# A hybrid transformer step on one Trainium2 core: one modulation vector's sums move from TensorE to VectorE, and the adaLN norms go over to whole tiles

## The chip, the cores and the metric

The kernel runs as one program on one core of a Trainium2 chip. A core has TensorE (matmuls into PSUM), VectorE, ScalarE, GpSimd and SyncE; each works through its own queue in order, and they wait for one another by semaphores. The metric is the device time of one execution in microseconds (us); lower is better. All data is fp32. A matmul of full precision is made of three passes over operands that are split into a high and a low part.

## The reference, cut to what matters

```python
for d in range(DEPTH):                                   # 2 layers, D_MODEL 1024
    mod = silu(c) @ w_mod[d] + b_mod[d]                  # 6 vectors of 1024, for each token group
    sa, ca, ga, sm, cm, gm = split(mod, 6)               # shift, scale, gate: mixer, then MLP
    h = rmsnorm(x, norm_mix[d]) * (1 + ca) + sa
    q, k, v, gb, gc, xin, u, vs = split(h @ w_in[d])
    x = x + ga * (concat(attention, conv, chunk_mlp) @ w_out[d])
    h = rmsnorm(x, norm_mlp[d]) * (1 + cm) + sm
    x = x + gm * (square(relu(h @ w_up[d])) @ w_down[d]) # hidden 4096
y = rmsnorm(x, norm_final)
```

There are two token groups, 128 context tokens modulated by `c_ctx` and 256 latent tokens modulated by `c`: 384 columns in all. A modulation vector is named here by layer and place in the split: (0, 3) is layer 0's MLP shift `sm`, (0, 5) its MLP gate `gm`.

## The kernel before, in words

Activations lie transposed: 1024 features are KT = 8 tiles `dt` of 128 partitions, by T = 384 tokens. `GROUPS` are the two token groups, columns 0 to 127 and 128 to 383.

**Weights.** `refill` loads a chunk of 128x1024 weights into `raw` (a ring of six buffers, which all streamed data shares), ScalarE rounds it to `whi`, VectorE subtracts to get `wlo` (four buffers each). `mm3` is one tile product in three matmuls: high by high, high by low, low by high. A chunk gives 24 matmuls of 384 columns.

**Order.** The four compute engines run in the order of the code. `tick()` is called after each `mm3`; side work is written as generators that yield a number of ticks (`WAIT`, one number for each layer) and are resumed when so many ticks have gone by. The order is thus fixed when the program is built, and an instruction whose data is late stops its engine.

**Modulation vectors.** Those in `MOD_PE` are made on TensorE by `mod_products`: 32 small matmuls `pm` of 256 columns for a vector, 8 of them in a step, then a transpose and `mod_done` on VectorE. Those in `MOD_DVE` are made on VectorE by `mod_sums`: `steps(sums, n, every)` issues n sums of 128x1024 (`junk`, with an accumulated result `mr`), one in `every` ticks, 16 for a vector; after the 16th comes `mod_done`.

**A layer.** Mixer: norm, input projections (`pkq`, then the 512 columns of `nat`, then `pgc`, `pxi`, `pgb`, `pk`, `pq`, `pu`), attention in twelve units (`sc` scores, `e` softmax, `pt` transposes, `po` values), output projection (`po2`). Then the MLP in two halves f = 0, 1: sixteen hidden tiles up (`pup`), eight output tiles down (`pdn`).

**Norms.** The first products of a norm run on x times scale, unnormed (`raw_x`, with two more columns that hold the shift: `shift_columns`), and `hidden` or `evict` multiplies by `rstd` afterwards. Meanwhile the true normed input (`normed_x`, tiles `nh`, `nl`, shown as `hh`, `hl`) is made tile by tile: in layer 1's mixer by `norm_part`, which calls `normed`, and during the down products of f = 0 by `normed_again`. For each tile VectorE makes `t` = x * scale * rstd in two instructions (one for each token group), ScalarE adds the shift and rounds into `hh` in two, VectorE makes the low part `hl` in two.

Of the kernel before, what the change touches and what calls it, by code (L numbers as in the profile page):

```python
# [21 lines left out]
T = TP + TS  # L22
# [13 lines left out]
    "sums_down": (6, 2),  # L36
    "hid0": (1, 3),
    "hid1": (3, 4),
    "later": (2, 3),
    "later2": (6, 6),  # L40
    "spread": (1, 1),
    "final": (4, 3, 3, 3),
# [9 lines left out]
    "at8": (1, 3),  # L52
    "at9": (2, 3),
    "at10": (3, 4),
    "at11": (3, 1),
    "at12": (1, 3),
    "k0": (1, 5),
    "k1": (8, 6),
# [9 lines left out]
    "cv1": (1, 2),  # L68
    "cv2": (2, 3),
    "cm0": (1, 1),  # L70
    "sy": (2, 1),
    "normed": (3, 3),
    "wait_normed": (13, 13),
    "mix": (6, 4),
# [1 line left out]
    "mods": (7, 0),  # L76
    "mods0": (5, 3),
    "sums": (7, 0),
    "sums0": (58, 1),
    "unit0": (24, 24),  # L80
    "head": (24, 24),
    "late": (0, 5),
# [2 lines left out]
GROUPS = ((0, 0, TP), (1, TP, T))  # L85
# [11 lines left out]
TE = T + 2  # L97
# [3 lines left out]
def dit_kernel(ctx, tc, xT, cT, wmod, wmodT, wall, wfirst, ck, cv, ws, lam, bs_in, small, rope, ident_in, yT, kT_out, v_out):  # L101
    nc = tc.nc
    const = ctx.enter_context(tc.tile_pool(name="const", bufs=1))
    wpool = ctx.enter_context(tc.tile_pool(name="wpool", bufs=1))
    work = ctx.enter_context(tc.tile_pool(name="work", bufs=2))
# [105 lines left out]
    def misc_tile(name="misc"):  # L211
        return ps.tile([P, 512], F32, tag="misc", name=name, bufs=3)

    def temp(name):
        return work.tile([P, T], F32, name=name, tag="tA", bufs=4)

    def mm3(out, w, a, wsl, asl, first, last):

# [110 lines left out]
    products = mod_products()  # L329
# [16 lines left out]
    def rsqrt_refined(y, a, ms):  # L346

        nc.vector.tensor_mul(a, y, y)
        nc.vector.scalar_tensor_tensor(a, a, -0.5, ms, ALU.mult, ALU.mult)
        nc.vector.scalar_tensor_tensor(y, a, 1.5, y, ALU.add, ALU.mult)  # L350

    def rstd_of_x():
        pm = misc_tile("pstat")
        mm(pm[:, 0:T], ones_d, stat["acc"], start=True, stop=True)
        y = stat["rstd"] = work.tile([P, T], F32, name="rstd", bufs=1)
        yield 2
        nc.scalar.activation(y, pm[:, 0:T], AF.Ln)
        nc.scalar.activation(y, y, AF.Exp, scale=-0.5)
        yield 2
        a = work.tile([P, T], F32, name="rtmp", tag="rtmp", bufs=1)  # L360
        rsqrt_refined(y, a, pm[:, 0:T])

    def normed(scale, shift, every):


        def times(dt):
            t = temp("t")
            for g, a, b in GROUPS:
                nc.vector.scalar_tensor_tensor(
                    t[:, a:b], x[:, dt, a:b], scale[:, dt, g : g + 1], stat["rstd"][:, a:b], ALU.mult, ALU.mult  # L370
                )
            return t

        t = times(0)
        for dt in range(KT):
            for g, a, b in GROUPS:
                nc.scalar.activation(nh[:, dt, a:b], t[:, a:b], AF.Identity, bias=shift[:, dt, g : g + 1])  # L377
            ahead = times(dt + 1) if dt + 1 < KT else None
            for g, a, b in GROUPS:
                nc.vector.scalar_tensor_tensor(  # L380
                    nl[:, dt, a:b], t[:, a:b], shift[:, dt, g : g + 1], nh[:, dt, a:b].bitcast(F32),
                    ALU.add, ALU.subtract,
                )
            t = ahead
            if dt + 1 < KT:
                yield every

    def normed_again(scale, shift, every):

        for dt in range(KT):  # L390
            t = temp("t")
            for g, a, b in GROUPS:
                nc.vector.scalar_tensor_tensor(
                    t[:, a:b], x[:, dt, a:b], scale[:, dt, g : g + 1], stat["rstd"][:, a:b], ALU.mult, ALU.mult
                )
            yield every[0]
            for g, a, b in GROUPS:
                nc.scalar.activation(nh[:, dt, a:b], t[:, a:b], AF.Identity, bias=shift[:, dt, g : g + 1])
            yield every[1]
            for g, a, b in GROUPS:  # L400
                nc.vector.scalar_tensor_tensor(
                    nl[:, dt, a:b], t[:, a:b], shift[:, dt, g : g + 1], nh[:, dt, a:b].bitcast(F32),
                    ALU.add, ALU.subtract,
                )
            yield every[2]

    def scaled_high(dt, scale, to=raw_x):
# [127 lines left out]
    for d in range(DEPTH):  # L535
# [125 lines left out]
        else:  # L661
# [10 lines left out]

            def norm_part():
                yield wt["wait_normed"]
                yield from normed(amix[d], modv[d][:, 0], wt["normed"])

            start(norm_part())
            for i in (2, 3):
# [229 lines left out]
        if d == 0:  # L908
            nc.sync.dma_start(bs, bs_in)
            for i in range(DEPTH):  # L910
                start(lambdas(i), 4 + 4 * i)
            start(steps(products, 3 * (KT // 2 + 1), wt["mods"]), wt["mods0"])
            start(steps(sums, 2 * KT, wt["sums"]), wt["sums0"])

        def units(h):
# [20 lines left out]
            chunk_mlp(ct)  # L936


        shift_columns(modv[d][:, 3])
        ya = (y[:, 0], y[:, 1])  # L940
        for i0 in range(0, KT, 2):
            outs = proj_tiles(ya, 2, T, "po2", (4, 5, 6, 0, 1, 2, 7, 3))
            for i in range(2):
                go(finish_x(i0 + i, outs[i], modv[d][:, 2], amlp[d]))

# [3 lines left out]
        for f in range(2):  # L949
            if d == 0:  # L950
                start(steps(sums, (16, 28)[f], (8, 4)[f]), 2)
            ah = wpool.tile([P, HALF, T], F32R, tag="hidH", name="ah")
            al = wpool.tile([P, HALF, T], F32R, tag="hidL", name="al")

            def hidden(i, pt, wait=0):
                if wait:
                    yield wait
                r = temp("relu")
                if f == 1:
                    nc.scalar.activation(r, pt[:, 0:T], AF.Relu)  # L960
                    nc.scalar.activation(r, r, AF.Square)
                    nc.scalar.copy(ah[:, i], r)
                    yield wt["hid1"]
                    nc.vector.tensor_sub(al[:, i], r, ah[:, i].bitcast(F32))
                    return
                ub = work.tile([P, 2], F32, name="ub")
                nc.vector.tensor_copy(ub, pt[:, T:TE])
                nc.vector.tensor_mul(r, pt[:, 0:T], stat["rstd"])
                yield wt["hid0"]
                for g, s0, s1 in GROUPS:  # L970
                    nc.scalar.activation(r[:, s0:s1], r[:, s0:s1], AF.Relu, bias=ub[:, g : g + 1])
                nc.scalar.activation(r, r, AF.Square)
# [12 lines left out]
            if f == 1 and not last:
                shift_columns(modv[d + 1][:, 0])
            if d == 0:
                start(steps(sums, (12, 24)[f], (9, 5)[f]), 2)
            if f == 0:
                start(normed_again(amlp[d], modv[d][:, 3], (2, 2, 12)), 3)  # L990

            def down(pt, w, c, cols):

                for k in range(8):
                    kt = c * 8 + k
                    mm3(pt[:, cols], w, (ah, al), (slice(None), slice(k * P, k * P + P)),
                        (slice(None), kt, cols), kt == 0, kt == HALF - 1)
                    tick()

            for dt in range(KT - 1 if last else KT):  # L1000
                pt = acc_tile("pdn")
                for c in range(2):
                    down(pt, chunk(), c, slice(0, T))
                    go(refill())
                go(finish_x(dt, pt, modv[d][:, 5], amix[d + 1] if f == 1 and not last else None, last))


    gate = modv[DEPTH - 1][:, 5]
    y = work.tile([P, T], F32, name="rstd", bufs=1)
    newton = work.tile([P, T], F32, name="rtmp", tag="rtmp", bufs=1)  # L1010

    def finish_part(dt, group, pt):
# [37 lines left out]

MOD_PE = ((0, 1), (0, 0), (0, 2), (0, 3), (0, 4))
MOD_DVE = ((0, 5), (1, 1), (1, 0), (1, 2), (1, 3), (1, 4), (1, 5))

_OUTS = [((KT, P, T), "float32"), ((DEPTH, NH, P, TP), "float32"), ((DEPTH, TP, 512), "float32")]

# [111 lines left out]
```

## Time and profile before

| | us |
|---|---|
| median of 3 runs (896.75 to 897.56) | 897.35 |
| the profiled execution | 896.73 |
| span of its records | 894.9 |
| TensorE busy in the span | 875.6 |
| VectorE busy | 657.3 |
| ScalarE busy | 485.7 |
| GpSimd busy | 82.8 |

An engine's busy time is the time in which at least one of its instructions runs. The profiled execution is 1.8 us longer than its span and 0.6 us shorter than the median. In the trace PE is TensorE, DVE VectorE, ACT ScalarE, POOL GpSimd.

### The profile page before, as it was taken

The page shows a single profiled execution, that of the slowest core. Times are in us where ns is not written, and L with a number is a line of the kernel's source. Part 1 is how long each engine was busy: PE and PEld are TensorE (multiplying, and loading weights), DVE is VectorE, ACT ScalarE, POOL GpSimd, SP SyncE. Part 2 cuts the span into 40 slices and gives each one's busy share as a digit, 9 for nine tenths or more (in the row PEclk, how much of TensorE's full clock was granted, in tenths as well). Part 3 has the DMA queues.
Part 4 walks back from the last instruction along what each step waited for, and adds up shares of the span by engine and source line. Part 5 has one row for each costly group of instructions (what it writes and reads, how often), then busy time and mean ns, then how long its engine had stood idle before and what let it go on. Part 6 is the DMA issues. An engine that isn't in the chain of part 4 may idle for free.

```text
span 894.9 us, 14560 instructions
## 1 busy us (share of the span) xinstructions
PE 875.6 (98%) x5502; PEld 840.4 (94%) x5502; DVE 657.3 (73%) x1218; ACT 485.7 (54%) x954; POOL 82.8 (9%) x85
## 2 busy tenths in 40 slices
PE   8999999999999999999999899999999999999996
PEld 6767889999999999999997799999999999999996
DVE  4699987889888779969979887568977554444332
ACT  4568775547654336554336786545765344565331
POOL 1015110020000000000112330002000000000022
PEclk9999999999999999999999999999999999999999
DMA  9976874455656558857663332233565343343302
GB/s 342 402 248 237 281 270 169 136 161 188 210 168 208 167 168 252 252 190 246 217 216 124 112 98 96 95 109 127 191 195 179 121 137 119 125 135 118 118 1 71
DMA packets 49046, 156.55 MB, mean 175 GB/s; under 512 B 5456, under 2 KB 11088, under 8 KB 48976
## 3 DMA queue, kind: packets, MB, share of 16 engines
q1 hardware_dynamic: 48432, 155.36, 52.5%
q8 instruction: 43, 0.70, 0.3%
q10 hardware_dynamic: 544, 0.26, 0.1%
q14 instruction: 27, 0.22, 0.1%
HBM read 152.98 MB, written 2.62 MB: 174 GB/s over the span
## 4 chain that ended last, share of the span: by engine, by line
PE 85%; DVE 6%; DMA 5%; issue 2%; ACT 1%; SPq 0%; POOL 0%; DVEq 0%; POOLq 0%; ACTq 0%
PE pdn L221 10%; PE pdn L220 10%; PE pdn L222 10%; PE pup L221 10%; PE pup L220 10%; PE pup L222 10%; PE po L221 2%; PE po L222 2%; PE po L220 2%; DMA raw<-in_wmod_dram 2%; PE po L823 1%; DVE wlo L203 1%; PE pm L264 1%; DVE hl L380 1%; DMA raw<-in_wall_dram 1%
## 5 line engine op out<-in xcount | busy, mean ns | idle before, releaser
L201 ACT CAST whi<-raw 128x1024 fp32r<-128x1024 f32 x182 | 190.0, 1050 | 276.0 <-PE pdn L221 114.0
L203 DVE TENSOR_TENSOR wlo<-raw,whi 128x1024 fp32r<-128x1024 f32 x182 | 222.8, 1230 | 80.2 <-ACT whi L201 80.0
L220 PE MATMUL pdn<-ah,whi 128*128 128x384 f32 (+2 forms) x528 | 174.9, 331 | 0.0
L221 PE MATMUL pdn<-al,whi 128*128 128x384 f32 (+2 forms) x528 | 174.8, 331 | 0.0
L222 PE MATMUL pdn<-ah,wlo 128*128 128x384 f32 (+2 forms) x528 | 174.8, 331 | 0.0
L220 PE MATMUL pup<-hh,whi 128*128 128x386 f32 (+1 forms) x512 | 173.7, 339 | 0.0
L221 PE MATMUL pup<-hl,whi 128*128 128x386 f32 (+1 forms) x512 | 172.8, 337 | 0.3
L222 PE MATMUL pup<-hh,wlo 128*128 128x386 f32 (+1 forms) x512 | 172.5, 337 | 0.0
L322 DVE SCALAR_TENSOR_TENSOR junk<-raw,cb 128x1024 bf16<-128x1024 f32 x112 | 136.5, 1219 | 0.7
L221 PEld LDWEIGHTS pdn<-al,whi 128*128 128x128 f32 x528 | 99.3, 188 | 0.0
L220 PEld LDWEIGHTS pdn<-ah,whi 128*128 128x128 f32 x528 | 99.2, 188 | 0.0
L222 PEld LDWEIGHTS pdn<-ah,wlo 128*128 128x128 f32 x528 | 99.3, 188 | 0.0
L221 PEld LDWEIGHTS pup<-hl,whi 128*128 128x128 f32 x512 | 96.5, 188 | 1.1 <-DVE hl L414 0.9
L220 PEld LDWEIGHTS pup<-hh,whi 128*128 128x128 f32 x512 | 96.2, 188 | 0.3
L222 PEld LDWEIGHTS pup<-hh,wlo 128*128 128x128 f32 x512 | 96.4, 188 | 0.0
L344 POOL TENSOR_TENSOR sacc<-sacc,sq 128x384 f32<-128x384 f32 x23 | 29.4, 1277 | 666.4 <-ACT sq L337 531.8
L425 DVE SCALAR_TENSOR_TENSOR x<-pdn,modv,x 128x128 f32<-128x128 f32 (+1 forms) x62 | 23.0, 413 | 46.8 <-PE pdn L222 46.6
L220 PE MATMUL po<-y,whi 128*128 128x384 f32 x128 | 43.1, 337 | 0.0
L222 PE MATMUL po<-y,wlo 128*128 128x384 f32 x128 | 42.8, 335 | 0.0
L221 PE MATMUL po<-y,whi 128*128 128x384 f32 x128 | 42.8, 334 | 0.0
L477 PE MATMUL nat<-whi,hl 128*128 128x512 f32 (+1 forms) x96 | 33.1, 345 | 2.4 <-DVE hl L380 2.3
L475 PE MATMUL nat<-whi,hh 128*128 128x512 f32 (+1 forms) x96 | 33.9, 354 | 0.5 <-ACT hh L377 0.5
(213 smaller groups left out, 1443.6 us busy)
## 6 DMA issues: line engine op xcount, KB each, us to landing
raw<-in_wall_dram SPq DMA_DIRECT2D x182, 512.0 KB, 3.6
raw<-in_wmodT_dram SPq DMA_DIRECT2D x56, 512.0 KB, 4.2
raw<-in_wmod_dram SPq DMA_DIRECT2D x40, 512.0 KB, 6.1
raws<-in_wfirst_dram SPq DMA_DIRECT2D x8, 256.0 KB, 7.4
x<-in_xT_dram SPq DMA_DIRECT2D x8, 192.0 KB, 6.5
raws<-in_wall_dram SPq DMA_DIRECT2D x2, 512.0 KB, 7.5
out_dram<-x SPq DMA_DIRECT2D x4, 256.0 KB, 2.3
mix<-in_cv_dram SPq DMA_DIRECT2D x2, 256.0 KB, 5.3
```

Of the source, the lines that this page charges most:

```text
L201: nc.scalar.copy(hi, r)
L203: nc.vector.tensor_sub(lo, r, hi.bitcast(F32))
L220: mm(out, wh[wsl], ah[asl], start=first, stop=False)
L221: mm(out, wh[wsl], al[asl], start=False, stop=False)
L222: mm(out, wl[wsl], ah[asl], start=False, stop=last)
L264: mm(pm[32 * j : 32 * j + 32, own], sct[:, kt, :], w[:, (4 * k + j) * width : (4 * k + j + 1) * width], start=(kt == 0), stop=(kt == KT - 1),)
L322: nc.vector.scalar_tensor_tensor(junk, w, 1.0, cb[:, g], ALU.mult, ALU.mult, accum_out=mr[:, dt, g : g + 1])
L344: eng.tensor_add(stat["acc"], stat["acc"], sq)
L380: nc.vector.scalar_tensor_tensor(nl[:, dt, a:b], t[:, a:b], shift[:, dt, g : g + 1], nh[:, dt, a:b].bitcast(F32), ALU.add, ALU.subtract,)
L425: nc.vector.scalar_tensor_tensor(x[:, dt, a:b], pacc[:, a:b], gate[:, dt, g : g + 1], x[:, dt, a:b], ALU.mult, ALU.add)
L475: mm(o, ah, wh[:, cols], start=(kt == 0 and tt % n == 0), stop=False)
L477: mm(o, al, wh[:, cols], start=False, stop=(kt == KT - 1 and (tt % n == n - 1 or tt == 2)))
```

## The change

(0, 3) goes from `MOD_PE` to the head of `MOD_DVE`. The sixteen sums that run during layer 0's mixer, (0, 5) before, are now (0, 3); (0, 5) moves to f = 0's up products, and layer 0's f = 0 down products carry 28 sums, one in 4 ticks, where they carried 12, one in 9. `shift_columns` for the MLP moves from before the output projection to after its third pair of tiles. `normed_again` and layer 1's mixer norm (`normed_whole`, new) multiply a whole tile by `rstd` on VectorE, apply scale and shift in place on ScalarE, round the whole tile there with one more instruction, and subtract the whole tile on VectorE. `hidden` takes the two shift columns through the same multiply as the tile (`rstd1`, with ones in its last two columns), without a copy of its own. Layer 0's mixer norm keeps `normed`.

```diff
-    "later": (2, 3),
+    "later": (2, 4),
-    "at11": (3, 1),
+    "at11": (4, 1),
-    "sy": (2, 1),
+    "sy": (4, 1),
...
-        y = stat["rstd"] = work.tile([P, T], F32, name="rstd", bufs=1)
+        stat["rstd1"] = work.tile([P, TE], F32, name="rstd", bufs=1)
+        nc.gpsimd.memset(stat["rstd1"][:, T:TE], 1.0)
+        y = stat["rstd"] = stat["rstd1"][:, 0:T]
...
+    def normed_whole(scale, shift, every):
+        def times(dt):
+            t = temp("t")
+            nc.vector.tensor_mul(t, x[:, dt], stat["rstd"])
+            return t
+
+        t = times(0)
+        for dt in range(KT):
+            for g, a, b in GROUPS:
+                nc.scalar.activation(
+                    t[:, a:b], t[:, a:b], AF.Identity, bias=shift[:, dt, g : g + 1], scale=scale[:, dt, g : g + 1]
+                )
+            nc.scalar.copy(nh[:, dt], t)
+            ahead = times(dt + 1) if dt + 1 < KT else None
+            nc.vector.tensor_sub(nl[:, dt], t, nh[:, dt].bitcast(F32))
+            t = ahead
+            if dt + 1 < KT:
+                yield every
...
-                yield from normed(amix[d], modv[d][:, 0], wt["normed"])
+                yield from normed_whole(amix[d], modv[d][:, 0], wt["normed"])
...
-            start(steps(products, 3 * (KT // 2 + 1), wt["mods"]), wt["mods0"])
+            start(steps(products, 2 * (KT // 2 + 1), wt["mods"]), wt["mods0"])
...
-        shift_columns(modv[d][:, 3])
...
+            if i0 == 4:
+                shift_columns(modv[d][:, 3])
...
-                ub = work.tile([P, 2], F32, name="ub")
-                nc.vector.tensor_copy(ub, pt[:, T:TE])
-                nc.vector.tensor_mul(r, pt[:, 0:T], stat["rstd"])
+                r = temp("relu", TE)
+                nc.vector.tensor_mul(r, pt[:, 0:TE], stat["rstd1"])
...
-                start(steps(sums, (12, 24)[f], (9, 5)[f]), 2)
+                start(steps(sums, (28, 24)[f], (4, 5)[f]), 2)
...
-                start(normed_again(amlp[d], modv[d][:, 3], (2, 2, 12)), 3)
+                start(normed_again(amlp[d], modv[d][:, 3], (2, 2, 10)), 3)
...
-MOD_PE = ((0, 1), (0, 0), (0, 2), (0, 3), (0, 4))
-MOD_DVE = ((0, 5), (1, 1), (1, 0), (1, 2), (1, 3), (1, 4), (1, 5))
+MOD_PE = ((0, 1), (0, 0), (0, 2), (0, 4))
+MOD_DVE = ((0, 3), (0, 5), (1, 1), (1, 0), (1, 2), (1, 3), (1, 4), (1, 5))
```

**TensorE, layer 0's mixer, at the products `pgc` of the second convolution tile.** Before:

```order
L221 MATMUL pgc<-hl,whi 128x384
L222 MATMUL pgc<-hh,wlo 128x384
L264 MATMUL pm<-raw,sct 32x256 x8
L220 MATMUL pgc<-hh,whi 128x384
L221 MATMUL pgc<-hl,whi 128x384
L222 MATMUL pgc<-hh,wlo 128x384
L800 MATMUL pt<-ident,e 128x128 x3
```

The same place in the changed kernel:

```order
L221 MATMUL pgc<-hl,whi 128x384
L222 MATMUL pgc<-hh,wlo 128x384
L220 MATMUL pgc<-hh,whi 128x384
L221 MATMUL pgc<-hl,whi 128x384
L222 MATMUL pgc<-hh,wlo 128x384
L818 MATMUL pt<-ident,e 128x128 x3
```

A step of eight `pm` is gone here. It is the first of the last vector's four steps: (0, 4) has moved up into the places that (0, 3) had, and the four places behind stand empty.

**VectorE, layer 0's MLP, down products of f = 0, from one output tile's residual (`x<-pdn`) to the next.** `t` and `hl` are the normed tile and its low part, `junk` is a sum. Before:

```order
L425 SCALAR_TENSOR_TENSOR x<-pdn,modv_91,x 128x128
L425 SCALAR_TENSOR_TENSOR x<-pdn,modv_91,x 128x256
L203 TENSOR_TENSOR wlo<-raw,whi 128x1024
L393 SCALAR_TENSOR_TENSOR t<-x,amlp_95,rstd 128x128
L393 SCALAR_TENSOR_TENSOR t<-x,amlp_95,rstd 128x256
L322 SCALAR_TENSOR_TENSOR junk,mr<-raw,cb 128x1024
L401 SCALAR_TENSOR_TENSOR hl<-t,modv_91,hh 128x128
L401 SCALAR_TENSOR_TENSOR hl<-t,modv_91,hh 128x256
L203 TENSOR_TENSOR wlo<-raw,whi 128x1024
L322 SCALAR_TENSOR_TENSOR junk,mr<-raw,cb 128x1024
```

In the changed kernel:

```order
L443 SCALAR_TENSOR_TENSOR x<-pdn,modv_91,x 128x128
L443 SCALAR_TENSOR_TENSOR x<-pdn,modv_91,x 128x256
L322 SCALAR_TENSOR_TENSOR junk,mr<-raw,cb 128x1024
L203 TENSOR_TENSOR wlo<-raw,whi 128x1024
L322 SCALAR_TENSOR_TENSOR junk,mr<-raw,cb 128x1024
L414 TENSOR_TENSOR t<-x,rstd 128x384
L322 SCALAR_TENSOR_TENSOR junk,mr<-raw,cb 128x1024
L203 TENSOR_TENSOR wlo<-raw,whi 128x1024
L422 TENSOR_TENSOR hl<-t,hh 128x384
L322 SCALAR_TENSOR_TENSOR junk,mr<-raw,cb 128x1024
```

Four sums stand between two residuals where one or two stood, and the norm's four instructions have become two.

**VectorE, layer 1's mixer, where the norm begins.** `mix` is an evicted key or query tile, `bias` its shift. Before:

```order
L546 TENSOR_TENSOR mix<-pkq,rstd 128x128
L546 TENSOR_TENSOR mix<-pkq,rstd 128x256
L203 TENSOR_TENSOR wlo<-raw,whi 128x1024
L369 SCALAR_TENSOR_TENSOR t<-x,amix_94,rstd 128x128
L369 SCALAR_TENSOR_TENSOR t<-x,amix_94,rstd 128x256
L369 SCALAR_TENSOR_TENSOR t<-x,amix_94,rstd 128x128
L369 SCALAR_TENSOR_TENSOR t<-x,amix_94,rstd 128x256
L380 SCALAR_TENSOR_TENSOR hl<-t,modv_92,hh 128x128
L380 SCALAR_TENSOR_TENSOR hl<-t,modv_92,hh 128x256
L667 COPY bias_4954<-pkq 128x2
L548 SCALAR_TENSOR_TENSOR mix<-pkq,rstd 128x384
```

In the changed kernel:

```order
L564 TENSOR_TENSOR mix<-pkq,rstd 128x128
L564 TENSOR_TENSOR mix<-pkq,rstd 128x256
L369 TENSOR_TENSOR t<-x,rstd 128x384 x2
L380 TENSOR_TENSOR hl<-t,hh 128x384
L203 TENSOR_TENSOR wlo<-raw,whi 128x1024
L685 COPY bias_4914<-pkq 128x2
L566 SCALAR_TENSOR_TENSOR mix<-pkq,rstd 128x384
```

Half of the norm's instructions are gone, and the chunk's `wlo` now stands behind the first finished tile instead of ahead of it.

## Rows read from the trace of the kernel before

**Rows 1.** The page's busy times: engine, us, share of the span, instructions.
```profile
span 894.9 us, 14560 instructions
...
PE 875.6 (98%) x5502; PEld 840.4 (94%) x5502; DVE 657.3 (73%) x1218; ACT 485.7 (54%) x954; POOL 82.8 (9%) x85
```

**Rows 2.** Stretches: length, each engine's busy time (instructions), clock, DMA share, GB/s.
```profile
60.00:84.00 24.00, 23.14 (x156) 17.17 (x155) 23.37 (x52) 19.78 (x49) 11.47 (x12) 1.00 0.72 251
...
110.00:135.00 25.00, 25.00 (x200) 21.68 (x199) 22.56 (x51) 17.67 (x48) 3.08 (x3) 1.00 0.72 271
...
260.40:327.00 66.60, 66.60 (x386) 66.60 (x385) 50.53 (x89) 25.61 (x36) 0.00 (x0) 1.00 0.58 179
327.00:393.80 66.80, 66.80 (x387) 66.80 (x386) 60.71 (x91) 38.26 (x61) 0.00 (x0) 1.00 0.76 238
...
480.00:510.00 30.00, 25.22 (x115) 19.47 (x114) 28.29 (x59) 23.29 (x54) 10.87 (x11) 1.00 0.32 100
```

**Rows 3.** TensorE's timeline around one step: start, us, line, tiles, form.
```profile
83.77 0.34 PE L779 MATMUL sc<-kl,qs 128*128 128x384 f32 x1
84.04 1.07 PE L264 MATMUL pm<-raw,sct 128*32 128x256 f32 x16
85.04 0.44 PE L220 MATMUL pxi<-hh,whi 128*128 128x384 f32 x1
85.32 0.34 PE L221 MATMUL pxi<-hl,whi 128*128 128x384 f32 x1
```

**Rows 4.** VectorE's groups by shape: count, busy us, mean ns, idle before.
```profile
L203 DVE TENSOR_TENSOR wlo<-raw,whi 128x1024 fp32r<-128x1024 f32 x182 | 222.8, 1230 | 80.2 <-ACT whi L201 80.0
L322 DVE SCALAR_TENSOR_TENSOR junk<-raw,cb 128x1024 bf16<-128x1024 f32 x112 | 136.5, 1219 | 0.7
L964 DVE TENSOR_TENSOR al<-relu,ah 128x384 fp32r<-128x384 f32 x32 | 17.9, 558 | 5.3 <-ACT ah L962 4.8
...
L393 DVE SCALAR_TENSOR_TENSOR t<-x,amlp,rstd 128x256 f32<-128x256 f32 x16 | 7.7, 480 | 0.0
...
L393 DVE SCALAR_TENSOR_TENSOR t<-x,amlp,rstd 128x128 f32<-128x128 f32 x16 | 5.5, 347 | 0.0
```

**Rows 5.** ScalarE's groups by shape, the same columns.
```profile
L201 ACT CAST whi<-raw 128x1024 fp32r<-128x1024 f32 x182 | 190.0, 1050 | 276.0 <-PE pdn L221 114.0 <-PE pup L221 79.2 <-issue 41.4
...
L973 ACT CAST ah<-relu 128x384 fp32r<-128x384 f32 x32 | 16.4, 514 | 1.0
```

**Rows 6.** VectorE's timeline in layer 0's first down products.
```profile
303.21 1.23 DVE L203 TENSOR_TENSOR wlo<-raw,whi 128x1024 fp32r<-128x1024 f32 x1 [0.21 <-ACT whi L201]
304.35 0.74 DVE L393 SCALAR_TENSOR_TENSOR t<-x,amlp,rstd 128x128 f32<-128x128 f32 x2
305.01 1.22 DVE L322 SCALAR_TENSOR_TENSOR junk<-raw,cb 128x1024 bf16<-128x1024 f32 x1
306.15 0.08 DVE L322 DVE_READ_ACCUMULATOR junk<-raw,cb 128x1 f32 x1
306.15 0.75 DVE L401 SCALAR_TENSOR_TENSOR hl<-t,modv,hh 128x128 fp32r<-128x128 f32 x2
```

**Rows 7.** VectorE's timeline in layer 0's output projection.
```profile
182.44 0.17 DVE L236 TENSOR_TENSOR modv<-mr,sm 128x16 f32<-128x16 f32 x1
...
191.40 1.39 DVE L425 SCALAR_TENSOR_TENSOR x<-po,modv,x 128x128 f32<-128x128 f32 x4 [1.78 <-PE po L222]
```

**Rows 8.** TensorE's timeline in layer 1's mixer: three waits.
```profile
485.43 0.50 PE L477 MATMUL nat<-whi,hl 128*128 128x512 f32 x1 [0.64 <-DVE hl L380]
...
491.57 0.51 PE L477 MATMUL nat<-whi,hl 128*128 128x512 f32 x1 [1.48 <-DVE hl L380]
...
504.20 0.33 PE L800 MATMUL pt<-ident,e 128*128 128x128 f32 x1 [1.42 <-DVE e L796]
```

**Rows 9.** VectorE's timeline in layer 1's mixer: pairs of norm instructions.
```profile
489.02 1.76 DVE L369 SCALAR_TENSOR_TENSOR t<-x,amix,rstd 128x128 f32<-128x128 f32 x2
...
492.98 0.75 DVE L369 SCALAR_TENSOR_TENSOR t<-x,amix,rstd 128x128 f32<-128x128 f32 x2
```

More of the change, by code (lines that the diff above doesn't have):

```diff
@@ L78 @@
     "sums": (7, 0),
-    "sums0": (58, 1),
+    "sums0": (58, 3),
     "unit0": (24, 24),
@@ L212, in misc_tile, with temp @@
         return ps.tile([P, 512], F32, tag="misc", name=name, bufs=3)
-    def temp(name):
-        return work.tile([P, T], F32, name=name, tag="tA", bufs=4)
+    def temp(name, cols=T):
+        return work.tile([P, TE], F32, name=name, tag="tA", bufs=4)[:, 0:cols]
     def mm3(out, w, a, wsl, asl, first, last):
@@ L391, in normed_again @@
             t = temp("t")
[L392 to L395, printed above, removed]
+            nc.vector.tensor_mul(t, x[:, dt], stat["rstd"])
             yield every[0]
             for g, a, b in GROUPS:
-                nc.scalar.activation(nh[:, dt, a:b], t[:, a:b], AF.Identity, bias=shift[:, dt, g : g + 1])
+                nc.scalar.activation(
+                    t[:, a:b], t[:, a:b], AF.Identity, bias=shift[:, dt, g : g + 1], scale=scale[:, dt, g : g + 1]
+                )
+            nc.scalar.copy(nh[:, dt], t)
             yield every[1]
[L400 to L404, printed above, removed]
+            nc.vector.tensor_sub(nl[:, dt], t, nh[:, dt].bitcast(F32))
             yield every[2]
@@ L957, in hidden @@
                     yield wait
-                r = temp("relu")
                 if f == 1:
+                    r = temp("relu")
                     nc.scalar.activation(r, pt[:, 0:T], AF.Relu)
@@ L965, in hidden @@
                     return
-                ub = work.tile([P, 2], F32, name="ub")
-                nc.vector.tensor_copy(ub, pt[:, T:TE])
-                nc.vector.tensor_mul(r, pt[:, 0:T], stat["rstd"])
+                r = temp("relu", TE)
+                nc.vector.tensor_mul(r, pt[:, 0:TE], stat["rstd1"])
                 yield wt["hid0"]
                 for g, s0, s1 in GROUPS:
-                    nc.scalar.activation(r[:, s0:s1], r[:, s0:s1], AF.Relu, bias=ub[:, g : g + 1])
+                    nc.scalar.activation(r[:, s0:s1], r[:, s0:s1], AF.Relu, bias=r[:, T + g : T + g + 1])
+                r = r[:, 0:T]
                 nc.scalar.activation(r, r, AF.Square)
@@ L1008, in dit_kernel @@
     gate = modv[DEPTH - 1][:, 5]
-    y = work.tile([P, T], F32, name="rstd", bufs=1)
+    y = work.tile([P, TE], F32, name="rstd", bufs=1)[:, 0:T]
     newton = work.tile([P, T], F32, name="rtmp", tag="rtmp", bufs=1)
```

## The prediction

> **What bounds the kernel now.** I read the page's busy times first. TensorE is busy 875.6 of 894.9 us, VectorE 657.3, ScalarE 485.7 [rows 1], so work taken off TensorE is worth its full length unless TensorE then waits for somebody. Where it would wait I read from the busy times by stretch [rows 2]. In layer 0's mixer (110 to 135 us) and in both halves of its MLP (the down products of f = 0 at 260.4 to 327, the up products of f = 1 behind them) TensorE has no idle time, with VectorE busy 90%, 76% and 91%. Where VectorE is busy 94% or more TensorE does wait: 0.86 us of 24 at 60 to 84, and 4.78 us of 30 at 480 to 510, layer 1's mixer while its norm is made. Three of those waits are the rows of TensorE's timeline: 0.64 and 1.48 us for the norm's low part `hl`, 1.42 us for an attention tile `e` [rows 8]. VectorE is late with both.
>
> **TensorE: the shift's four steps.** A step of eight `pm` stands between two ordinary products. In TensorE's timeline the last product ahead of it starts at 83.77, the second one behind it at 85.32 [rows 3]. Products follow each other every 0.173 us (66.6 us at full pace [rows 2] hold 16 chunks of 24), so without the step that distance would be two products, 0.35 us. It is 1.55: a step costs 1.20 us. It is more than the 1.07 us of its row, because the first product behind it takes 0.28 us to the next. Four steps: **-4.8 us**, all in stretches where TensorE never idles. The vector's eight loads stay, in `wmodT`'s form and in `raw`'s ring; their number over the kernel is the same.
>
> **VectorE in layer 0's mixer: the sums stay, the time shrinks.** The sixteen sums there belong to another vector, but stand in the same places. The four empty places lie at about 112 to 132 us. VectorE's 22.56 us of work in 110 to 135 [rows 2] must now fit into 25 - 4.8 = 20.2 us: it falls up to 2.4 us behind. The attention tiles are issued some ticks ahead of their use, and a tick (three products) is 0.52 us, so most of the lag should stay hidden. Bounds 0 and +2.4; I take **+0.4**. `sy` and `at11`, two ticks and one later, let VectorE stand less behind ScalarE's roundings; I give them nothing.
>
> **Shift columns.** (0, 3)'s sums end where (0, 5)'s ended, at 182.44 [rows 7]. The columns' low part now stands right behind that on VectorE and waits for ScalarE, which first does two casts `whi` of 1.05 us [rows 5] that wait for TensorE's chunk. Queued behind it are the four residuals, two `wlo` and four low parts of that pair of tiles, all about 2 us later. The cover is the 1.78 us that VectorE idles before the residuals at 191.40 [rows 7], so 0.2 us is left over, ahead of the MLP's first products: **+0.2**; without the cover 2.0.
>
> **VectorE in layer 0's f = 0 down products.** Here the sums grow from 12 to 28. By start to start in VectorE's timeline a `wlo` takes 1.14 us, a pair of norm instructions 0.66, a sum 1.14 to 1.22 with its accumulator read [rows 6]; I take 1.18. A duration is 0.08 us longer than the step to the next start (0.74 against 0.66), so a whole tile, which the change makes with the kind of instruction of the row `al`, 558 ns [rows 4], takes 0.475. Added: 16 x 1.18 = 18.9. Saved: 8 tiles, two pairs each, 16 x (0.66 - 0.475) = 3.0. VectorE goes from 50.5 to 66.4 us of work in 66.6: full. I still cost it at nothing. There are four buffers of `whi` and `wlo`; a cast starts when TensorE leaves a chunk, and its result is wanted three chunks later, 3 x 4.16 = 12.5 us, less 1.05 for the cast and 1.14 for `wlo`. So VectorE may lag 10 us, and its excess is less: with four sums for an output tile of 8.3 us it needs 2.28 + 0.66 + 1.09 + 4.72 = 8.75 us, 0.4 too much, seven times: 3 us, given back in the last tile, which has few sums. If TensorE paid as it does at 60 to 84 us (3.6%), it would be +2.4. The f = 1 up products already carry as many sums and wait for nothing at 91% [rows 2]. ScalarE gets one more rounding of 0.51 us [rows 5] for each tile, 4.1 us on 25.6 busy of 66.6. The gate (0, 5) is complete after 2 + 15 x 8 = 122 of the up products' 128 ticks and wanted 16 ticks into the down products: in time.
>
> **Layer 1's mixer norm.** VectorE saves the same 3.0 us, more where an instruction is stretched: of two like pairs one took 1.76 us, the other 0.75 [rows 9]. The moved `wlo` lets the first tile start 1.1 us earlier. Against that ScalarE's chain for each tile grows by the rounding, 8 x 0.51 = 4.1 us, between `t` and `hl`; it has 6.7 us of idle time in this stretch, partly spent waiting for `t`. Walking through the queues by these steps, the first five tiles come in time, and tile 5 and tile 7 still come late, because VectorE stands behind ScalarE (evicted keys and queries wait there behind the new roundings). About two thirds of the waits stay. Bounds: all 4.8 us won, or 4.1 - 3.0 = 1.1 lost. I take **-1.1**.
>
> **At nothing:** the memsets of `rstd1` (GpSimd has nothing to do there), the shift copies dropped in `hidden` (VectorE isn't waited for in those up products), layer 1's norm in the MLP (VectorE has room there).
>
> **Sum.** -4.8 + 0.4 + 0.2 - 1.1 = -5.3. From the profiled 896.73 that is 891.4; the median of the runs lies 0.6 above the profiled execution, so **892.0**.
>
> **The rivals.** *B, the layer 1 stage is freed.* If VectorE is all that holds it, its 4.8 us of waits go and not 1.1: 892.0 - 3.7 = 888.3. For it speaks that all three waits shown are for VectorE; against it, that ScalarE grows by 4.1 us. What stretches VectorE there coincides with GpSimd's 10.87 us of work in this stretch [rows 2, 9]; the long pair takes 1.0 us more than the short one, and four pairs of the stage are about so long. If each instruction can be held up once, half as many instructions halve that, 2 us more off VectorE, and B becomes likelier. (The Trainium skill, SBUF - State Buffer, section on SBUF's two separate sides, says that VectorE with two SBUF inputs and GpSimd lock each other out of a shared port for a whole instruction. The stretched pair agrees; by that rule alone the stage would give 3.1 us, 890.0 in all.)
>
> *C, VectorE eats it in layer 0.* The mixer lag is paid in full (+2.0 more than taken), the full down stage costs 2.4, and layer 1 gives half of what I took: 892.0 + 2.0 + 2.4 + 0.5 = 896.9, no change.
>
> *D, the other side: the sums overload the f = 0 down stage.* If TensorE waits there as it does at 480 to 510 us, where VectorE is 94% busy and TensorE stands 16% of the time, it pays 10.6 us of 66.6: 892.0 + 10.6 = 902.6. It goes this way if ScalarE, in order, waits for late `t` with the casts behind it, and VectorE then for the casts: the excess per tile would be 1.5 us and not 0.4, and pass the 10 us of slack. It decides from 7.1 us on, 0.9 for each of the eight tiles. Against it: at 480 to 510 a wait is on the norm's own data, here on weights loaded ahead.
>
> That the change doesn't happen is ruled out by the order of instructions: the four steps are gone.
>
> **How the numbers follow.** The likeliest case, 0.66, is 892.0, by itself 890.0 to 894.5. B 0.17, C 0.10, D 0.07. The range reaches to B at 888.3 and into C at 896.0; D and the end of C are left out. Runs of this kernel differ by 0.1% to either side, so 0.2%, 1.8 us, is about what can be told from no change: faster means under 895.5. That holds for the first two cases, 0.83; C is the same, 0.10; D slower, 0.07.
>
> **What would show it.** Right: between 110 and 135 us (earlier by what has been saved) no `pm` and no TensorE wait over 0.5 us; the down products of f = 0 still 66.6 us long with VectorE near 99%; in layer 1's mixer fewer and shorter waits for `hl`, ScalarE busier. Wrong: TensorE waits for `wlo` in the f = 0 down products or the up products behind; waits for `hh` or `e` in layer 1 as long as before; or TensorE waits in layer 0's attention that add up to the steps removed.

## The result, and the profile after

The changed kernel takes 892.46 us (median of 4 runs, 891.85 to 893.69), the kernel before 897.36 beside it (896.75 to 897.56): a ratio of 0.9945, 95% interval 0.9933 to 0.9956, 4.9 us. The forecast was 892.0. The profiled execution is the longest of the four, 893.69 us, with a span of 890.9. Its busy times stand in the page as follows.

```profile
span 890.9 us, 14470 instructions
...
PE 871.3 (98%) x5438; PEld 838.9 (94%) x5438; DVE 659.8 (74%) x1169; ACT 499.0 (56%) x978; POOL 87.3 (10%) x89
```

TensorE has 4.3 us less to do than in [rows 1], VectorE 2.5 more, ScalarE 13.3 more. By stretches, in the columns of [rows 2]:

```profile
110.00:132.00 22.00, 21.79 (x145) 21.45 (x144) 21.34 (x52) 16.87 (x45) 4.06 (x4) 1.00 0.46 151
257.40:324.00 66.60, 66.60 (x386) 66.60 (x386) 64.28 (x106) 29.95 (x45) 0.00 (x0) 1.00 0.72 233
...
474.90:506.50 31.60, 27.59 (x127) 21.48 (x126) 27.45 (x51) 29.30 (x66) 13.90 (x13) 1.00 0.35 115
```

Layer 0's mixer is full on both engines. In the f = 0 down products VectorE is busy 64.28 of 66.60 us, and TensorE has no idle time. In layer 1's mixer ScalarE is now the busiest engine, 29.30 of 31.60. Of the waits left to TensorE, these are from its timeline:

```profile
131.10 0.55 PE L818 MATMUL pt<-ident,e 128*128 128x128 f32 x3 [0.21 <-DVE e L814]
195.44 0.44 PE L221 MATMUL pup<-hl,whi 128*128 128x386 f32 x1 [0.38 <-DVE hl L432]
...
482.23 0.50 PE L495 MATMUL nat<-whi,hl 128*128 128x512 f32 x1 [0.44 <-DVE hl L380]
...
493.40 0.50 PE L493 MATMUL nat<-whi,hh 128*128 128x512 f32 x1 [1.62 <-ACT hh L378]
...
500.21 0.33 PE L818 MATMUL pt<-ident,e 128*128 128x128 f32 x1 [1.45 <-DVE e L814]
...
617.33 0.44 PE L221 MATMUL pup<-hl,whi 128*128 128x386 f32 x1 [0.36 <-DVE hl L432]
```

Beside [rows 8], the longest wait for the norm is no longer for VectorE's `hl` but for ScalarE's `hh`. The waits at 195.44 and 617.33, the first products of each layer's MLP, are new.

Added up, the waits for layer 1's norm are no shorter: 0.64, 1.48 and 0.17 us in the kernel before, 0.44, 0.16, 0.20 and 1.62 now. Gone is a wait that [rows 8] left out, for ScalarE's `e` in the scores (TensorE's timeline, before):

```profile
500.07 0.45 PE L778 MATMUL sc<-kh,qs 128*128 128x384 f32 x1 [0.92 <-ACT e L788]
```

`e` needs the row maxima `nm` of the scores, which stand on VectorE behind the norm's last `hl`. VectorE's timeline before, then in the changed kernel:

```profile
495.77 1.77 DVE L380 SCALAR_TENSOR_TENSOR hl<-t,modv,hh 128x128 fp32r<-128x128 f32 x2
...
499.25 0.47 DVE L783 TENSOR_REDUCE nm<-sc 128x1 f32<-128x128 f32 x2
```

```profile
493.38 0.57 DVE L380 TENSOR_TENSOR hl<-t,hh 128x384 fp32r<-128x384 f32 x1 [2.06 <-ACT hh L378]
...
495.23 0.48 DVE L801 TENSOR_REDUCE nm<-sc 128x1 f32<-128x128 f32 x2
```

A span is too coarse for what follows, so each trace was cut at the first product of a name in TensorE's timeline. The columns: start (to layer 0's first `nat`), M0 (from there to the first `pu`), U0 (first `pup` to first `pdn`), D (f = 0's down products), U1 (f = 1's up products), N1 (layer 1's first `nat` to the next `po`), nm (from that `nat` to VectorE's first `nm` behind it), V1 (layer 1's first `pup` to `pdn`), all (first `nat` to the last norm's statistics). Us.

| kernel | start | M0 | U0 | D | U1 | N1 | nm | V1 | all |
|---|---|---|---|---|---|---|---|---|---|
| before | 50.29 | 94.33 | 68.72 | 66.58 | 66.77 | 40.62 | 21.33 | 68.72 | 831.78 |
| changed | 51.31 | 89.97 | 68.99 | 66.57 | 66.77 | 39.64 | 20.36 | 68.97 | 826.93 |
| move_only | 51.18 | 90.48 | 68.98 | 66.58 | 66.76 | 40.63 | 21.33 | 68.97 | 828.45 |
| norms_only | 51.12 | 94.32 | 68.72 | 66.58 | 66.76 | 39.67 | 20.37 | 68.73 | 830.81 |
| waits_back | 50.78 | 90.51 | 69.01 | 66.57 | 66.77 | 39.63 | 20.36 | 68.99 | 827.52 |
| shift_late | 51.88 | 89.99 | 68.75 | 66.57 | 66.77 | 39.65 | 20.36 | 68.72 | 826.48 |
| extra8 | 50.33 | 90.01 | 68.98 | 68.95 | 68.22 | 39.68 | 20.36 | 69.01 | 830.88 |
| extra16 | 51.42 | 89.98 | 68.99 | 77.82 | 68.25 | 39.66 | 20.36 | 68.98 | 839.71 |
| l1_direct | 50.86 | 89.95 | 69.00 | 66.57 | 66.76 | 37.94 | 18.67 | 69.00 | 825.24 |
| l1_round_vec | 51.48 | 90.00 | 69.01 | 66.57 | 66.77 | 40.22 | 20.96 | 68.99 | 827.59 |
| l1_mixed | 51.04 | 89.96 | 68.76 | 66.57 | 66.77 | 39.42 | 20.15 | 68.75 | 826.27 |
| l1_tile7 | 51.01 | 90.00 | 68.75 | 66.58 | 66.76 | 40.01 | 20.74 | 68.73 | 826.86 |
| l1_every2 | 50.79 | 89.96 | 68.75 | 66.57 | 66.77 | 40.85 | 20.93 | 68.75 | 827.70 |

A stage that a kernel doesn't edit repeats within 0.06 us; the start, which no edit touches, varies by 1.6. So the 1.02 us that the changed kernel's profiled start is longer says nothing of the change, and from the first `nat` on it is 831.78 - 826.93 = 4.85 us shorter: M0 -4.36, U0 +0.27, N1 -0.98, V1 +0.25. N1 is `nm` and 19.26 to 19.32 us in every kernel but `l1_every2` (19.92): the first scores' `e` and, behind it, the first `pt` wait for `nm`, and so the moment at which VectorE gets to it sets the stage, whatever TensorE waits for ahead of that.

### The profile page after: what moved, and what is told of

Read it like the earlier page. It is cut to its first block, busy times and chain, and to the rows that moved or that the text cites. A ratio compares the mean times of both kernels' runs of the same rounds, so it can differ in the third digit from the quotient of the medians.

```text
span 890.9 us, 14470 instructions
## 1 busy us (share of the span) xinstructions
PE 871.3 (98%) x5438; PEld 838.9 (94%) x5438; DVE 659.8 (74%) x1169; ACT 499.0 (56%) x978; POOL 87.3 (10%) x89
## 4 chain that ended last, share of the span: by engine, by line
PE 80%; DVE 8%; DMA 4%; issue 4%; ACT 3%; POOL 0%; SPq 0%; DVEq 0%; ACTq 0%; POOLq 0%
PE pdn L221 10%; PE pdn L220 10%; PE pdn L222 10%; PE pup L221 10%; PE pup L220 10%; PE pup L222 10%; DVE wlo L203 2%; DMA raws<-in_wfirst_dram 2%; DMA raw<-in_wmod_dram 1%; PE po L220 1%; PE po L221 1%; PE po L222 1%; PE po L841 1%; DVE hl L432 1%; PE pkq L220 1%
## 5 line engine op out<-in xcount | busy, mean ns | idle before, releaser
L322 DVE SCALAR_TENSOR_TENSOR junk<-raw,cb 128x1024 bf16<-128x1024 f32 x128 | 156.0, 1219 | 0.8
L344 POOL TENSOR_TENSOR sacc<-sacc,sq 128x384 f32<-128x384 f32 x23 | 31.4, 1367 | 660.1 <-ACT sq L337 530.2
L443 DVE SCALAR_TENSOR_TENSOR x<-pdn,modv,x 128x128 f32<-128x128 f32 (+1 forms) x62 | 23.0, 412 | 33.3 <-PE pdn L222 33.2
```

The source lines that it names most:

```text
L322: nc.vector.scalar_tensor_tensor(junk, w, 1.0, cb[:, g], ALU.mult, ALU.mult, accum_out=mr[:, dt, g : g + 1])
L344: eng.tensor_add(stat["acc"], stat["acc"], sq)
L443: nc.vector.scalar_tensor_tensor(x[:, dt, a:b], pacc[:, a:b], gate[:, dt, g : g + 1], x[:, dt, a:b], ALU.mult, ALU.add)
```

## The experiments

### The parts alone

`move_only`, against the kernel before, leaves the norms and the two spacings as they were:

```diff
-            start(steps(products, 3 * (KT // 2 + 1), wt["mods"]), wt["mods0"])
+            start(steps(products, 2 * (KT // 2 + 1), wt["mods"]), wt["mods0"])
-        shift_columns(modv[d][:, 3])
+            if i0 == 4:
+                shift_columns(modv[d][:, 3])
-                start(steps(sums, (12, 24)[f], (9, 5)[f]), 2)
+                start(steps(sums, (28, 24)[f], (4, 5)[f]), 2)
-MOD_PE = ((0, 1), (0, 0), (0, 2), (0, 3), (0, 4))
+MOD_PE = ((0, 1), (0, 0), (0, 2), (0, 4))
```

> The kernel before with the move alone: (0, 3) to VectorE, 28 sums in layer 0's f = 0 down products, shift columns after the third pair; norms, hidden and the spacings sy and at11 as before. Theory (the move pays by itself, and the down stage has slack): the mixer stages of layer 0 from the first nat product to the first po product are 4.3 us shorter, as in the changed kernel, each layer's first up products lose 0.25 us to the shift columns, layer 1's nat stage stays at 22.6 us; VectorE has 69.4 us of work for the 66.6 us of the f = 0 down products and lags some 5 us at most, under the 10 us of slack, so the stage stays at 66.6 us. In all about -3.8 us, near 893.5. Rival (the whole-tile norms are needed to make room for the sums): TensorE waits for wlo in the f = 0 down products or the up products behind, 2 us or more, and the total is 895.5 or more.

`norms_only` is the rest without the spacings `sy` and `at11`: `normed_whole`, `normed_again` in whole tiles with its spacing of 10, `rstd1`, `later` 4.

> The kernel before with the whole-tile norms, the hidden tiles' shift columns and the spacing later = 4 alone; (0, 3) stays on TensorE. Theory: layer 1's stage from the first nat product to the first pk product is 1.0 us shorter (22.6 to 21.6) and nothing else moves: -1.0 us, near 896.3, at the edge of what can be told. Rival 1: nothing in that stage moves without the move of (0, 3) (0.0 in all). Rival 2: the norms also shorten the first up products of a layer or layer 0's down products (they have no TensorE wait to give), -2 us or more.

`waits_back`, against the changed kernel:

```diff
-    "at11": (4, 1),
+    "at11": (3, 1),
-    "sy": (4, 1),
+    "sy": (2, 1),
```

> The changed kernel, with the two spacings of layer 0's attention back at their values before (at11 at 3 ticks for 4, sy at 2 for 4). Theory: they are worth nothing; layer 0's mixer stages from the first nat to the first po product take 101.9 us as in the changed kernel, within 0.3 us. Rival: VectorE, with its work pressed into 4.8 us less, stands behind ScalarE's roundings, TensorE waits for e or chunk-MLP tiles, and 0.5 to 2 us of the 4.3 us come back.

Measured: `move_only` 893.93 us, ratio 0.9959 (0.9944 to 0.9974); `norms_only` 896.63, ratio 0.9991 (0.9982 to 0.9999); `waits_back` in one run 892.77. By the table the move gives 3.33 us, the norms 0.97, all of it in N1, and `waits_back` loses 0.59, 0.54 of it in M0. The three sum to 4.89, the whole change to 4.85: they add up. The norms are not needed for the move, since D and U1 are as long in `move_only` as before. How much of the 0.97 is due to `later`, and how the spacings share theirs, no run shows. The spacings, expected to be worth nothing, are worth half a microsecond, as the rival had it at its low end. With them undone, TensorE's timeline has one longer wait in layer 0's attention:

```profile
131.10 0.55 PE L818 MATMUL pt<-ident,e 128*128 128x128 f32 x3 [0.74 <-DVE e L814]
```

It is the wait of 0.21 us of the changed kernel; the 0.53 us between them is the difference in M0. In VectorE's timeline of `waits_back`, the scaling of `e` stands ready 0.74 us early and waits for ScalarE, because the short operations that ScalarE waits for come behind a tile of 0.61 us:

```profile
128.75 0.61 DVE L867 SCALAR_TENSOR_TENSOR y<-pot,subg,y 128x384 fp32r<-128x384 f32 x1
129.28 0.15 DVE L810 RECIPROCAL s<-s 128x2 f32<-128x2 f32 x1
...
130.43 0.62 DVE L814 SCALAR_TENSOR_TENSOR e<-e,s 128x384 f32<-128x384 f32 x1 [0.74 <-ACT e L812]
```

In the changed kernel `at11`, one tick later, puts that `y` behind the reciprocal. So what a full VectorE costs here hangs on the order of two instructions.

### The shift columns

`shift_late`, against the changed kernel:

```diff
-            if i0 == 4:
-                shift_columns(modv[d][:, 3])
             for i in range(2):
                 go(finish_x(i0 + i, outs[i], modv[d][:, 2], amlp[d]))
+            if i0 == 4:
+                start(once(shift_columns, modv[d][:, 3]), 6)
```

> The changed kernel, with the shift columns of the MLP started 6 ticks after the third pair's residuals instead of ahead of them, in both layers. Theory (VectorE, behind the columns' low part that waits for ScalarE's two casts, is late with the first hl of the MLP): the waits of 0.38 and 0.36 us for hl at the first up products go, and the stage from the first up to the first down product falls by 0.25 us in each layer, to 68.7 us. Rival (the residuals themselves or rstd hold the first up products): both stages stay at 69.0. In the total, 0.5 us cannot be told; the stages are to be read.

U0 and V1 go back to 68.75 and 68.72: the theory holds. The total, 893.47 us in one run, is no lower; the run has the longest start of the table (last section). In VectorE's timeline of the changed kernel the columns' low part (L439) holds up the residuals (L443), of both layers:

```profile
181.76 0.18 DVE L439 TENSOR_TENSOR hl<-modv,hh 128x16 fp32r<-128x16 f32 x1 [2.47 <-ACT hh L438]
181.86 1.39 DVE L443 SCALAR_TENSOR_TENSOR x<-po,modv,x 128x128 f32<-128x128 f32 x4
...
603.68 0.18 DVE L439 TENSOR_TENSOR hl<-modv,hh 128x16 fp32r<-128x16 f32 x1 [3.83 <-ACT hh L438]
```

In `shift_late` it stands behind that pair's `wlo` and low parts and waits for nothing:

```profile
180.34 1.39 DVE L443 SCALAR_TENSOR_TENSOR x<-po,modv,x 128x128 f32<-128x128 f32 x4 [0.47 <-PE po L222]
...
186.80 0.16 DVE L439 TENSOR_TENSOR hl<-modv,hh 128x16 fp32r<-128x16 f32 x1
```

### How much the f = 0 down products still hold

`extra8` and `extra16`, against the changed kernel, differ in two numbers (8 and 14; 16 and 7):

```diff
+    def extra_sums():
+        er = work.tile([P, 32], F32, name="er", bufs=1)
+        for i in range(32):
+            junk = work.tile([P, DM], mybir.dt.bfloat16, name="junk", bufs=1)
+            nc.vector.scalar_tensor_tensor(
+                junk, cb[:, 0], 1.0, cb[:, 1], ALU.mult, ALU.mult, accum_out=er[:, i : i + 1]
+            )
+            yield
...
+            if d == 0 and f == 0:
+                start(steps(extra_sums(), 8, 14), 4)
```

> The changed kernel with eight more sums of 128x1024 on VectorE in layer 0's f = 0 down products (one in 14 ticks, on data that lies in SBUF already; their results are not used). VectorE then has 64.3 + 8 x 1.18 = 73.7 us of work for 66.6 us of products: 7 us too much. Theory (four buffers of whi and wlo give some 10 us of slack): the stage stays at 66.6 us, and the lag is worked off in the f = 1 up products, which may give up at most 1 us; total within 1 us of the changed kernel, 891.9 to 893.5. Rival (D of the prediction: no slack, TensorE pays for VectorE's overload as it comes): the stage takes 73 us or more, total 899 or more.

> The same with sixteen more sums, one in 7 ticks: VectorE has 64.3 + 16 x 1.18 = 83.2 us of work for 66.6 us, 16.6 us too much. Theory (10 us of slack): the lag passes the slack by 6 to 7 us and TensorE waits so long in all, for wlo, late in this stage or at the head of the f = 1 up products: total 898 to 900. Rival without slack: 16.6 us, 908 to 910. If the lag were free at any size (weights made far ahead), the total would stay at 892.5.

Measured in one run each: 896.31 and 905.61 us. D and U1 together lose 3.83 and 12.73 us; none of the numbers expected fits. `extra8` waits three times in TensorE's timeline:

```profile
307.20 0.45 PE L222 MATMUL pdn<-ah,wlo 128*128 128x384 f32 x1 [0.31 <-DVE wlo L203]
...
316.91 0.44 PE L222 MATMUL pdn<-ah,wlo 128*128 128x384 f32 x1 [0.70 <-DVE wlo L203]
...
327.09 0.44 PE L222 MATMUL pup<-hh,wlo 128*128 128x384 f32 x1 [1.19 <-DVE wlo L203]
```

The mistake is in where the expectation began. It set VectorE's whole work against the stage's length, idle time included, and took the 10 us of slack as untouched. But in the changed kernel VectorE's only idle times over 0.15 us in D, 0.72 and 0.34 us, lie at its start, ahead of the extra sums. What counts is the lead: how long before its first use a `wlo` is ready. For the first chunk of f = 1, the `wlo` ends in the kernel before at 315.69 + 1.23 = 316.92 us and is used at 327.36 (VectorE's and TensorE's timelines):

```profile
315.69 1.23 DVE L203 TENSOR_TENSOR wlo<-raw,whi 128x1024 fp32r<-128x1024 f32 x1 [0.47 <-ACT whi L201]
```

```profile
327.36 0.34 PE L222 MATMUL pup<-hh,wlo 128*128 128x384 f32 x1
```

That is a lead of 10.4 us, the slack that the prediction worked out from four buffers. In the changed kernel it is 324.30 - (317.60 + 1.22) = 5.5:

```profile
317.60 1.22 DVE L203 TENSOR_TENSOR wlo<-raw,whi 128x1024 fp32r<-128x1024 f32 x1
```

```profile
324.30 0.34 PE L222 MATMUL pup<-hh,wlo 128*128 128x384 f32 x1
```

So 5.0 us are spent already, and no chunk of D or U1 has a shorter lead. Eight sums at the 1.14 us from start to start of [rows 6] are 9.1, less 5.5: 3.6 (measured 3.83). Sixteen are 18.2: 12.7 (measured 12.73). In these two runs TensorE pays VectorE's work beyond the lead one for one.

### Who holds layer 1's norm

`l1_direct`, against the changed kernel:

```diff
-                    t[:, a:b], t[:, a:b], AF.Identity, bias=shift[:, dt, g : g + 1], scale=scale[:, dt, g : g + 1]
+                    nh[:, dt, a:b], t[:, a:b], AF.Identity, bias=shift[:, dt, g : g + 1], scale=scale[:, dt, g : g + 1]
                 )
-            nc.scalar.copy(nh[:, dt], t)
```

> The changed kernel, with layer 1's mixer norm leaving out ScalarE's rounding copy: scale and shift are written straight into the rounded tile nh, eight copies of 0.51 us fewer; the low part is then made from the unscaled tile, so that part of the computation is changed. Theory (ScalarE holds the stage since the change): the waits of TensorE for hh and hl, 2.4 us in the changed kernel, mostly go: the nat stage falls from 21.6 to 20 us or less, total 1 to 2 us lower, 890.5 to 891.5. Rival (VectorE still holds it, through the port it shares or its queue): stage and total stay within 0.4 us.

`l1_round_vec`: the copy only `if dt < 4`, and behind `ahead` for the others `nc.vector.tensor_copy(nh[:, dt], t)`.

> The changed kernel, with the rounding of tiles 4 to 7 of layer 1's mixer norm on VectorE and not on ScalarE: four copies of 0.51 us leave ScalarE, which is busy 29.3 of 31.6 us there, and come to VectorE, which is busy 27.5. Theory (ScalarE holds): the wait of 1.62 us for hh shrinks to about half, the nat stage is 0.5 to 1 us shorter. Rival (VectorE holds, or the two are level): the waits move to hl and the stage is the same or longer by up to 1 us.

Measured in one run each: 890.55 and 893.56 us; N1 37.94 and 40.22 against 39.64. In `l1_direct` the low part is made from the unscaled tile, so it leaves out a part of the norm's arithmetic. Without the copies 1.70 us go, and `nm` comes 1.69 us earlier. TensorE's wait of 1.62 us goes too, but one of 0.86 us for `e` comes back in the scores. So ScalarE's copies hold the stage by way of the last `hl`, for which VectorE waits 2.06 us ahead of `nm`; TensorE's own wait for `hh` is not what counts. Half of the copies on VectorE cost 0.58: `nm` comes 0.60 us later. VectorE's timeline in `l1_round_vec` has the copy at two prices, the first beside an instruction of GpSimd (486.42 to 487.34), the second beside none:

```profile
486.68 0.88 DVE L382 CAST hh<-t 128x384 fp32r<-128x384 f32 x1
...
490.11 0.35 DVE L382 CAST hh<-t 128x384 fp32r<-128x384 f32 x1
```

Three attempts to share the load better, all with `shift_late`'s edit: `l1_mixed` (tiles 3 and 7 as in the kernel before), `l1_tile7` (tile 7's copy alone on VectorE) and `l1_every2` (`normed` 2 ticks for 3 in layer 1).

> The changed kernel with the shift columns started late (as above) and tiles 3 and 7 of layer 1's mixer norm in the form of before: ScalarE has two roundings of 0.51 us fewer, VectorE two pairs more for whole tiles, 2 x 0.4 us. Theory (the two engines are about level, and ScalarE holds tile 7): the wait of 1.62 us for tile 7's high part shrinks to some 1.1, the nat stage is 0.3 to 0.7 us shorter than 21.6. Rival (what leaves one engine is paid on the other, as where tiles 4 to 7 were rounded on VectorE, 22.2 us): 21.6 or more.

> The changed kernel with the shift columns started late and tile 7 alone rounded on VectorE, which idles 2.06 us there while it waits for ScalarE's rounding. Theory (the copy took 0.35 us on VectorE where nothing held it up, 0.51 on ScalarE): the wait for tile 7 is 0 to 0.4 us shorter, the nat stage 21.2 to 21.6 us, nothing else moves. Rival: the copy is held up to 0.9 us there, as two of the four were, and the stage is 0.2 to 0.4 us longer.

> The changed kernel with the shift columns started late and two ticks instead of three between the tiles of layer 1's mixer norm, so that tile 7's work on ScalarE stands ahead of more of the keys' and queries' work. Theory (tile 7 is late because of what stands ahead of it in ScalarE's order): its wait of 1.62 us shrinks by half or more, the nat stage is 0.5 to 1.5 us shorter; the keys and queries come later, and the first attention unit's wait for e, 1.45 us, may take up to 0.5 us of it back. Rival (ScalarE is simply full, 29.3 of 31.6 us): what is won before the scores is lost at e, and from the first nat product to the first po product nothing changes (39.6 us).

Measured: 891.76, 892.33 and 892.97 us in one run each; N1 39.42, 40.01 and 40.85. `l1_mixed` wins 0.22, less than expected: the wait for tile 7 is gone, but one of 0.92 us for an attention tile `e` comes up behind it, and `nm` is only 0.21 us earlier. `l1_tile7` loses 0.37 where 0 to 0.4 less was expected: the copy takes 0.89 us on VectorE, as its rival had it, `nm` comes 0.38 us later, and from the first `nat` to the first `pk` it takes 23.5 us for 21.6. `l1_every2` loses 1.21: there TensorE waits for no part of the norm, but for the queries' low part and for `e`. In both, TensorE's clock fell as well (last section).

### The best of these

`best` is `l1_mixed`, timed in rounds.

> The same kernel as in the run with tiles 3 and 7 in the form of before, timed in rounds. By the stages it stands at 826.27 us from layer 0's first nat product to the last norm's statistics, the changed kernel at 826.93, the one before at 831.78. Theory (the stages repeat, what varies between runs is the start): 5.5 us under the kernel before, a ratio of 0.9939, 891.7 us against 897.2. Rival (the stage gains were of that one run): no more than the changed kernel's ratio, 0.9945 to 0.995.

It took 892.07 us (5 runs, 891.31 to 892.41), ratio 0.9943 (0.993 to 0.9957). Its stages sum to 826.20 from the first `nat` on, 0.73 below the changed kernel's, so they repeat; the interval can't tell it from the changed kernel.

## Why the prediction was right

**The four steps, -4.8.** Right, to the step. From first product to first product in TensorE's timelines, the second `pgc` tile takes 5.31 us for 6.53, `pxi` 6.56 for 7.79, `pgb` with its two steps 5.21 for 7.54: 1.22, 1.23 and 2.33, in all 4.78, at 1.20 a step.

**VectorE in layer 0's mixer, +0.4.** M0 is 4.36 shorter and not 4.78, so 0.42 was paid, 0.38 of it between the last `nat` products and the first `pu`, where the `pt` wait of 0.21 stands. The value was a choice between 0 and 2.4, and it was right only together with the two spacings, which the prediction gave nothing: without them it is 0.96. That it fits so closely is luck.

**Shift columns, +0.2.** The mechanism held, with 0.27 measured. The term was mis-sized by leaving out layer 1, where the same edit stands behind a wait of 3.83 us and costs 0.25.

**The f = 0 down products, 0.** Right: 66.57 us. The slack of 10 us is the lead of 10.4 in the kernel before. VectorE's work was put at 66.4 us and is 64.28, yet the lag, put at 3 us, is 5.0 at the first chunk of f = 1; what makes it larger was not taken apart. Rival D is ruled out here, but not far: by the two points of `extra8` and `extra16`, VectorE could take four more sums in this stage before TensorE pays.

**Layer 1's mixer norm, -1.1.** Measured 0.98, in N1, but not on the path that the prediction took, so the close number is luck. It let a third of TensorE's waits go. The waits for the norm did not shrink (2.29 us before, 2.42 now), and the wait for `e` at the first `pt` is as long as before, 1.45 us for 1.42, which the prediction had named as a sign of being wrong. Tile 7 is late by 1.62 us, tile 5 only by 0.16 and 0.20, and tile 3, which the walk through the queues had in time, by 0.44. What sets the stage is VectorE's `nm`, which the prediction doesn't mention. It comes 0.97 us earlier: the last `hl` ends 0.55 us earlier, counted from the first `nat`, and the `qs` behind it takes 0.87 us for 1.29.

Rival B failed for the reason given against it: VectorE's norm instructions fell from 17.7 us in this stage to 11.9 (sums of their durations by group), yet TensorE gained 1.0, because VectorE now waits for ScalarE. `l1_direct` shows what the eight copies cost, 1.7 us; without them N1 is 2.68 us shorter than before, and not 4.8.

**Rival C**, VectorE eats it, would have needed M0 to lose 2 us more and D 2.4; neither did.

The sum of these terms as measured is -4.78 + 0.42 + 0.27 + 0.25 - 0.98 = -4.82, against -5.3 forecast, and the medians differ by 4.9. The omitted layer 1 columns are half of the 0.5.

## What to carry to other kernels

Before more work goes to an engine that looks nearly full, measure its lead over the consumer, buffer by buffer: in these runs work up to the lead was free and work beyond it was paid one for one, and VectorE's busy time, 64.28 of 66.60 us, told neither. When an engine is relieved, look at once for the next in line: here 5.8 us of VectorE's work went out of a stage and 1.0 us came of it, because VectorE then waited for ScalarE. The longest wait need not be on the path: TensorE's 1.62 us for tile 7 went in `l1_mixed` and the stage became only 0.22 us shorter, while the place of `nm` on VectorE told its length in twelve of thirteen kernels. In a full in-order queue, the place of one instruction of 0.2 us that waits for another engine cost 0.25 us in each layer, together half of what the rewritten norm brings.

## What the hardware showed

TensorE's granted clock fell to 0.50 (1.2 GHz) at the end of waits of 2.02 to 2.55 us or soon behind them. `l1_tile7`, TensorE's timeline and then the stretches:

```profile
493.30 0.50 PE L496 MATMUL nat<-whi,hh 128*128 128x512 f32 x1 [2.02 <-DVE hh L382]
```

```profile
493.30:494.40 1.10, 1.10 (x3) 0.72 (x4) 1.04 (x3) 1.05 (x1) 0.00 (x0) 0.82 0.25 101
494.40:496.97 2.57, 2.57 (x8) 1.99 (x7) 2.53 (x6) 1.51 (x6) 1.60 (x2) 0.50 0.00 0
```

In `l1_every2` it fell behind a wait of 2.19 us, with one of 1.59 soon after, and in `extra16` at the end of one of 2.26 us:

```profile
496.00:499.60 3.60, 3.54 (x11) 3.54 (x12) 2.99 (x6) 2.64 (x9) 1.60 (x1) 0.50 0.36 129
```

```profile
308.10:311.20 3.10, 3.04 (x9) 3.04 (x10) 3.06 (x7) 0.18 (x1) 0.00 (x0) 0.50 0.48 169
```

In the start of `shift_late` it fell at the end of a wait of 2.55 us, which belongs to no edit (TensorE's timeline and the stretch):

```profile
14.65 0.69 PE L220 MATMUL pkq<-hh,whi 128*128 128x384 f32 x1 [2.55 <-ACT hh L428]
```

```profile
15.00:18.00 3.00, 3.00 (x68) 2.23 (x67) 0.81 (x2) 0.63 (x2) 0.00 (x0) 0.50 1.00 385
```

Behind the 1.62 and 1.45 us of the changed kernel it stayed at 1.00 (the stretch from 474.90 above). In `l1_tile7` the wait grew by only 0.4 us, from 1.62 to 2.02, and the products behind it took 0.43 us from start to start for 0.23. It lost only 0.37 us in all, because the wait of 1.45 us for `e` that follows in the changed kernel was gone: TensorE came that much later.

Most of VectorE's whole-tile instructions of the norm take about 0.55 or about 1.10 us in layer 1's mixer, here in the changed kernel, where GpSimd's timeline has an instruction running from 475.78 to 476.89:

```profile
475.74 0.55 DVE L369 TENSOR_TENSOR t<-x,rstd 128x384 f32<-128x384 f32 x1
476.20 1.10 DVE L380 TENSOR_TENSOR hl<-t,hh 128x384 fp32r<-128x384 f32 x1
```

```profile
475.78 1.11 POOL L712 TENSOR_TENSOR rt<-mix,rp 128x256 f32<-128x256 f32 x1 [14.94 <-ACT mix L761]
```

The first started before GpSimd's and took 0.55 us, the second started beside it and took 1.10. The Trainium skill, SBUF — State Buffer, section on SBUF's two separate sides, says that whichever of the two starts first keeps the shared port for its whole instruction; a delay to 476.89 and then 0.55 us would end at 477.44, and the next instruction starts at 477.23, so the trace agrees roughly, as far as GpSimd's times can be trusted.
